# Experts of a mixture layer: weight splits and a step's small operations in program order on ScalarE and VectorE

## The chip, the cores and the metric

The kernel runs on one core of a Trainium2 chip. The metric is the time of one execution on the device, in microseconds (us); of several runs the median is given. TensorE is called PE here, VectorE DVE, ScalarE ACT, GpSimd POOL and SyncE SP, as in the profile; PEld is PE's loading of weights.

## The reference

A network of two blocks on 256 tokens of width 1024: in each a mixer (retention, then banded attention), a feed-forward part and a small per-layer embedding. The first feed-forward part is dense. The second, with which the change deals, is a mixture of eight experts with 3584 hidden columns, of which each token uses two:

```python
logits = (xn @ w_router).astype(jnp.float32)
top_v, top_i = lax.top_k(logits, TOP_K)
top_w = jax.nn.softmax(top_v, axis=-1)
gates = jnp.sum(jax.nn.one_hot(top_i, N_EXPERTS) * top_w[..., None], axis=-2)
for e in range(N_EXPERTS):
    y = y + gates[..., e:e + 1] * swiglu(xn, w_gate[e], w_up[e], w_down[e])
# swiglu: (silu(x @ w_gate) * (x @ w_up)) @ w_down
```

Inputs, weights and output are float32.

## The kernel before, in words

**Weights and their splits.** PE multiplies in a format of fewer bits than float32, so each operand is split into a high and a low part, and a product is the sum of three products (`mm3`, L341 to L345): high by high, low by high, high by low. All weights come as one stream (class `Stream`). Its chunks of 1 MB are loaded by SP into raw buffers (`wraw`): four at first, and `widen` adds three and then four more, so eleven in the experts. Each chunk makes two parts of 128 x 1024. A part is split by `_split` (L277 to L295): ACT copies the raw values into `whi` (L288), and DVE subtracts that from the raw values into `wlo` (L289). Five pairs of split buffers (`HL = 5`) are there. The last expert's parts are split in two halves of 128 x 512.

`get` (L297 to L306) is called for the chunks that the next matmuls need. It gives out splits until the part that stands five behind the first part asked for has its turn, so that splits run ahead of use:

```python
        while self.n_hl < min(max(end, at + self.hl_bufs), len(self.parts)):
            self._split()
```

**An expert.** `experts` (L997 to L1093) runs over experts 0 to 7 and, in each, over 14 steps j of 256 hidden columns. The tokens of an expert are first gathered into slots. A *wide* expert (0, 2, 3, 5, 6) has 128 slots, and its products are those three. A *narrow* expert (1, 4, 7) has 64 slots, whose high and low parts stand beside each other as 64 + 64 columns of one operand, so two products per weight do (L1012, L1013). A step does this:

1. Up product: two chunks (`eu`, four parts) into a PSUM bank `mm`, gate and up columns side by side; 24 matmuls in a wide expert, 16 in a narrow one.
2. Down product of the step before: one chunk (`ed`, two parts) into the two `acc` banks; 12 or 8 matmuls.
3. `turned` (L1025 to L1056). Wide: ACT's silu into `sg` (L1031), DVE's multiplication (L1032), two transposes on PE into `tp` (L1038), and a split of the result into `hh` (ACT, L348) and `hl` (DVE, L349), by `split_psum`. Narrow: ACT copies the bank into `cp` (L1043), PE folds high and low halves by eight small matmuls into `tp` (L1048), ACT's silu (L1052), DVE's multiplication (L1053) into `sgn`, and the split, both halves into one tile `hh`.

The split (with the silu, in a narrow expert) is held back as the closure `split` and called in the next step, behind the first call of `get` there (L1061 to L1064). At step 13 the tokens of the next pair of experts may be gathered, the last two down chunks are used, and the sum goes back to the tokens, weighted by the gates (L1082 to L1093).

**What sets the order.** The program's text gives each instruction a priority by its place, and the framework's planner orders each engine's instructions: among those that by its own timetable can run it takes the earliest in the program. That timetable is made before the kernel runs, and the order of each engine is fixed by it; on the chip an engine runs its instructions in that order and waits by semaphores. `after` (L443 to L445) adds a dependence without a semaphore: it only forces the planner to place one instruction behind another. SP's queue holds the loads, which `fill` issues as raw buffers come free; POOL has next to nothing to do in the experts.

By the program's text a step's order on ACT and DVE is this, with p and p+1 for the two parts of the down chunk of step j-1: the splits up to p+4, then `cp` or `sg` of step j, then splits p+5 and p+6 (the next `get`), then the held-back closure of step j. Parts p+2 to p+5 are up parts of step j+1 and p+6 and p+7 the down parts of step j.

Of the kernel before, what the change touches and what calls it, by code (L numbers as in the profile page):

```python
# [11 lines left out]
F32 = mybir.dt.float32  # L12
# [4 lines left out]
ALU = mybir.AluOpType  # L17
# [210 lines left out]
class Stream:  # L228


    def __init__(self, prog, plans, raw_bufs, hl_bufs, raw_pool, hl_pool):
        self.nc = prog.nc
        self.items, self.parts, self.first = [], [], []
        for ap, plan in plans:
            offs, _ = offsets(plan)
            for c, o in zip(plan, offs):
                self.first.append(len(self.parts))
                step = max(c.kt // 2, 1)
                self.parts += [(len(self.items), k, step) for k in range(0, c.kt, step)]
                self.items.append((ap, c, o))  # L240
        self.expert = prog.expert
        self.first.append(len(self.parts))
        self.free = {raw_pool: raw_bufs}
        self.base, self.extra = raw_pool, []
        self.hl_pool, self.hl_bufs = hl_pool, hl_bufs
        self.raw, self.hl = {}, {}
        self.n_raw = self.n_hl = self.n_get = 0
# [29 lines left out]
    def _split(self):  # L277
        i, k, nk = self.parts[self.n_hl]
        c = self.items[i][1]
        self.fill()  # L280
        t, pool = self.raw[i]
        f = nk * c.n
        hi, lo = (self.hl_pool.tile([P, 1024], F32R, name=n) for n in ("whi", "wlo"))
        n = 1 if c.key[0] in ("eu", "ed") and c.key[1] < NE - 1 else 2
        for i0 in range(0, f, f // n):
            h, l = (x[:, i0:i0 + f // n] for x in (hi, lo))
            src = t[:, k * c.n + i0:k * c.n + i0 + f // n]
            self.nc.scalar.activation(h, src, AF.Copy)  # L288
            self.nc.vector.tensor_tensor(l, src, h.bitcast(F32), op=ALU.subtract)  # L289
        if k + nk == c.kt:  # L290
            self.free[pool] += 1
            del self.raw[i]
        self.hl[self.n_hl] = [x[:, :f].rearrange("p (k n) -> p k n", n=c.n) for x in (hi, lo)]
        self.n_hl += 1
        self.fill()  # L295

    def get(self, *keys):  # L297

        at = self.first[self.n_get]
        for key in keys:  # L300
            assert self.items[self.n_get][1].key == key, (self.items[self.n_get][1].key, key)
            self.n_get += 1
        end = self.first[self.n_get]
        while self.n_hl < min(max(end, at + self.hl_bufs), len(self.parts)):
            self._split()
        return [[x[:, k, :] for x in self.hl[i]] for i in range(at, end) for k in range(self.parts[i][2])]  # L306


class Program:
    RAW, HL = 4, 5  # L310

    def __init__(self, tc, io, stop=None, dump=None):
        self.tc, self.nc, self.io = tc, tc.nc, io
        self.stop, self.dump_ap = stop, dump
        self.fence, self.in_set = [], []
        self.turns = {}
        self.expert = {}


# [24 lines left out]
        mm(out, l[0], r[1], start=False, stop=False)  # L344
        mm(out, l[1], r[0], start=False, stop=stop)  # L345

    def split_psum(self, hi, lo, ps):
        self.nc.scalar.activation(hi, ps, AF.Copy)  # L348
        self.nc.vector.tensor_tensor(lo, ps, hi.bitcast(F32), op=ALU.subtract)  # L349

    def gain_row(self, ap, n=D, name="gain", pool=None, engine=None):
        t = (pool or self.gains).tile([P, n], F32, name=name)
# [644 lines left out]
    def experts(self, px, pool, gates, slot, w, first, wide):  # L997
# [5 lines left out]
        for e in range(NE):  # L1003
# [21 lines left out]
            def turned(j, ps):  # L1025


                hh = pool.tile([P, 2, P], F32R, name="hh", bufs=2)
                if wide[e]:
                    sg = self.work.tile([P, 256], F32, name="sg", tag="xs", bufs=3)  # L1030
                    nc.scalar.activation(sg, ps[:, :256], AF.Silu)  # L1031
                    nc.vector.tensor_tensor(sg, sg, ps[:, 256:], op=ALU.mult)  # L1032
                    hT[j] = (hh, pool.tile([P, 2, P], F32R, name="hl", bufs=2))

                    def turn():
                        tp = self.bank("tp")
                        for k in range(2):
                            nc.tensor.transpose(tp[:, k * P:(k + 1) * P], sg[:, k * P:(k + 1) * P], self.ident)  # L1038
                        return lambda: self.split_psum(*hT[j], tp[:, :256].rearrange("p (k s) -> p k s", k=2))
                    return turn  # L1040
                hT[j] = (hh,)
                cp = self.work.tile([P, 512], F32, name="cp", tag="xs", bufs=3)
                nc.scalar.activation(cp, ps, AF.Copy)  # L1043

                def turn():
                    tp = self.bank("tp")[:, :256].rearrange("p (c s) -> p c s", s=64)
                    for c in range(4):
                        nc.tensor.matmul(tp[:, c], cp[:, c * P:(c + 1) * P], self.fold, start=True, stop=True)  # L1048

                    def split():  # L1050
                        sg = self.work.tile([P, 2, 64], F32, name="sgn", tag="xs", bufs=3)
                        nc.scalar.activation(sg, tp[:, :2], AF.Silu)  # L1052
                        nc.vector.tensor_tensor(sg, sg, tp[:, 2:], op=ALU.mult)  # L1053
                        self.split_psum(hh[:, :, :64], hh[:, :, 64:], sg)
                    return split
                return turn  # L1056

            split = None
            for j in range(nj):
                ps = self.bank("mm")  # L1060
                for k0 in (0, 4):  # L1061
                    wu = w.get(("eu", e, j, k0 * P))
                    if split:
                        split()  # L1064
                        split = None
                    for k in range(4):
                        product(ps, [a[:, k0 + k, :] for a in xg], wu[k],
                                k0 + k == 0, k0 + k == KD - 1)
                rows = rows_of(j - 1) if 0 < j < nj - 1 else []
                if j == nj - 1:  # L1070
                    if e + 1 in groups:
                        have.update(self.gather(px, pool, slot, groups[e + 1], wide))
                    rows = rows_of(nj - 2, nj - 1)
                    turn = turned(j, ps)
                    down(rows[:2])
                    turn()()
                    down(rows[2:], True)
                else:
                    turn = turned(j, ps)
                    down(rows)  # L1080
                    split = turn()
            with self.tc.high_priority(offset=300) if e == NE - 1 else nullcontext():  # L1082
                for n in range(2):
                    spare = n and e == NE - 1
# [10 lines left out]
    def moe_layer(self):  # L1095
        nc, tc, io = self.nc, self.tc, self.io
        with self.pool("moex") as px, self.pool("moe") as pool:
            with self.banks(acc="67", mm="45", tp="01", ps="23"):
                rows = [px.tile([P, NB, D], F32, name="xg", tag="xgl"), px.tile([P, KD, T], F32, name="xnT", tag="xgh")]
                with self.banks(mm="45", tp="45"):  # L1100
                    quarter = self.ple_up(1, self.pl1, pool)
                    for n in range(2):
                        quarter(0, n)
                with tc.high_priority(offset=300):
                    slot, weigh = self.router(*rows)
                    first = self.gather(px, pool, slot, GROUPS[0], WIDE)
                with tc.issue_after(self.logits.ins):
                    quarter(1, 0)
                    quarter(1, 1)
                gates, slot, load = weigh()  # L1110
                self.lb = self.lower_bounds(pool)
                most = nc.values_load(load[0:1, 0:1], min_val=0, max_val=P + T)
                self.experts(px, pool, gates, slot, self.w, first, WIDE)
        self.wide.close()
        with tc.If(most > P):
            with self.pool("moe2") as pool, self.pool("raw2", 2) as raw, \
                    self.pool("hl2", 4) as hl, self.banks(acc="67", mm="45", tp="01", ps="23"):
                again = Stream(self, [(self.we, plan_expert(i)) for i in range(NE)], 2, 4, raw, hl)
                nc.vector.tensor_tensor(slot, slot, self.turn[:, None, 1].to_broadcast([P, NB, NE]), op=ALU.subtract)
                wide = (True,) * NE  # L1120
                self.experts(pool, pool, gates, slot, again, self.gather(pool, pool, slot, GROUPS[0], wide), wide)
        self.routed.close()
        return self.at("e")

# [487 lines left out]
```

## Time and profile before

| | |
|---|---|
| median of 3 runs | 2432.98 us (2430.64 to 2434.96) |
| profiled execution | 2430.28 us, its span 2428.5 us, granted clock of PE 0.996 |
| PE busy | 2369.9 us, 98% of the span |
| DVE busy | 1892.6 us, 78% |
| ACT busy | 1567.7 us, 65% |
| weight load (PEld) busy | 1972.4 us, 81% |
| DMA | 605.72 MB, 249 GB/s over the span |
| experts | from about 575 to 1538 us of the span |

Busy shares are averages over stages with different limits, so a stage is read by its own stretch. An idle time of an engine has a releaser: the instruction of another engine, or the DMA, whose end let it go on. A matmul's end is modelled; from one matmul's start to the next is the better measure. In the timeline a row may stand for several instructions of one kind in a row (x2), and the time is then that of all.

### The profile page before, as it was taken

The numbers are of one execution on the slowest core, as the hardware profiler recorded it, in microseconds if no ns is written. First come the engines' busy times: TensorE is split into PE (matmuls) and PEld (weight loads), VectorE is DVE, ScalarE is ACT, GpSimd is POOL, SyncE is SP. The second block draws the span as 40 slices with busy tenths as digits, with TensorE's granted clock in tenths as the row PEclk, the third lists the DMA queues.
The fourth block names the chain that finished last, engine by engine and source line by source line (L and its number), as shares of the span: only waits on it lengthen the run. The fifth ranks groups of instructions, "written<-read, shape, count | busy, mean of one in ns | idle before, by whom it ended". The sixth has DMA issues, their size and how long they took to land. (4 is left out here: it accounts for less than half of the span.)

```text
span 2428.5 us, 35659 instructions
## 1 busy us (share of the span) xinstructions
PE 2369.9 (98%) x13032; PEld 1972.4 (81%) x13032; DVE 1892.6 (78%) x3026; ACT 1567.7 (65%) x2609; POOL 61.1 (3%) x105
## 2 busy tenths in 40 slices
PE   8999999999999999999999999899999999999999
PEld 6978998887876787876788876698789989878998
DVE  6756567778999889899998899878776567877655
ACT  6446555667888777778777789645755554575554
POOL 0000000000000000000000000100000000100000
PEclk9999999999999999999999999999999999999999
DMA  7445555567989998999999999534345554434553
GB/s 286 167 174 208 191 191 191 194 247 265 369 333 394 360 359 335 359 356 409 356 369 343 364 356 393 148 132 161 133 167 199 189 173 139 170 126 177 194 189 107
DMA packets 88393, 605.72 MB, mean 249 GB/s; under 512 B 10480, under 2 KB 12144, under 8 KB 17296
## 3 DMA queue, kind: packets, MB, share of 16 engines
q1 hardware_dynamic: 85792, 593.91, 65.4%
q0 software_dynamic: 2416, 9.44, 1.7%
q8 instruction: 104, 1.70, 0.3%
q14 instruction: 81, 0.66, 0.1%
HBM read 602.26 MB, written 1.05 MB: 248 GB/s over the span
## 5 line engine op out<-in xcount | busy, mean ns | idle before, releaser
L289 DVE TENSOR_TENSOR wlo<-wraw,whi 128x512 fp32r<-128x512 f32 (+1 forms) x1656 | 1383.4, 876 | 369.4 <-ACT whi L288 356.1
L288 ACT ACTIVATE whi<-wraw 128x512 fp32r<-128x512 f32 (+1 forms) x1656 | 1204.1, 776 | 438.9 <-PE mm L344 201.9
L343 PE MATMUL mm<-xth,whi 128*128 128x256 f32 x1296 | 366.3, 283 | 0.0
L345 PE MATMUL mm<-xth,wlo 128*128 128x256 f32 x1296 | 364.0, 281 | 1.2 <-DVE wlo L289 1.2
L344 PE MATMUL mm<-xtl,whi 128*128 128x256 f32 x1296 | 364.2, 281 | 0.0
L345 PEld LDWEIGHTS mm<-xth,wlo 128*128 128x128 f32 x1296 | 247.1, 191 | 2.1 <-DVE wlo L289 1.4
L343 PEld LDWEIGHTS mm<-xth,whi 128*128 128x128 f32 x1296 | 243.6, 188 | 4.9 <-issue 3.0
L344 PEld LDWEIGHTS mm<-xtl,whi 128*128 128x128 f32 x1296 | 243.8, 188 | 3.7 <-issue 2.1
L344 PE MATMUL acc<-wlo,hh 128*128 128x512 f32 x624 | 243.6, 390 | 0.0
L345 PE MATMUL acc<-whi,hl 128*128 128x512 f32 x624 | 243.5, 391 | 0.0
L343 PE MATMUL acc<-whi,hh 128*128 128x512 f32 x624 | 231.6, 391 | 1.5 <-ACT hh L348 1.5
L343 PE MATMUL mm<-whi,xth 128*128 128x512 f32 (+2 forms) x592 | 231.7, 391 | 0.6 <-ACT whi L288 0.4
L344 PE MATMUL mm<-wlo,xth 128*128 128x512 f32 (+2 forms) x592 | 231.5, 391 | 0.3 <-DVE wlo L289 0.3
L345 PE MATMUL mm<-whi,xtl 128*128 128x512 f32 (+2 forms) x592 | 229.5, 388 | 0.5 <-DVE xtl L349 0.5
L343 PE MATMUL mm<-whi,xgh 128*128 128x512 f32 x560 | 226.2, 404 | 2.6 <-ACT whi L288 2.6
L344 PE MATMUL mm<-wlo,xgh 128*128 128x512 f32 x560 | 223.8, 400 | 3.0 <-DVE wlo L289 3.0
L345 PE MATMUL mm<-whi,xgl 128*128 128x512 f32 x560 | 222.2, 397 | 0.0
L1013 PE MATMUL mm<-wlo,xgh 128*128 128x512 f32 x336 | 143.2, 426 | 5.2 <-DVE wlo L289 4.4
L343 PEld LDWEIGHTS acc<-whi,hh 128*128 128x128 f32 x624 | 117.1, 188 | 26.4 <-ACT hh L348 3.3
L345 PEld LDWEIGHTS acc<-whi,hl 128*128 128x128 f32 x624 | 117.1, 188 | 25.0 <-DVE hl L349 0.6
L344 PEld LDWEIGHTS acc<-wlo,hh 128*128 128x128 f32 x624 | 117.2, 188 | 23.4 <-DVE wlo L289 0.3
L1012 PE MATMUL mm<-whi,xgh 128*128 128x512 f32 x336 | 134.4, 400 | 0.0
(386 smaller groups left out, 3091.7 us busy)
## 6 DMA issues: line engine op xcount, KB each, us to landing
wraw<-in_we_dram SPq DMA_DIRECT2D x336, 1024.0 KB, 5.8
wraw<-in_w_dram SPq DMA_DIRECT2D x218, 1024.0 KB, 4.8
wraw<-in_w_dram SPq DMA_DIRECT2D x4, 912.0 KB, 4.7
wraw<-in_w_dram SPq DMA_DIRECT2D x6, 512.0 KB, 3.6
bias<-in_rel_rows_dram POOLq DMA_DIRECT2D x4, 768.0 KB, 4.6
gain<-in_norm_ffn_dram POOLq DMA_DIRECT2D x2, 512.0 KB, 6.6
gn<-in_ret_gn_dram SPq DMA_DIRECT2D x4, 256.0 KB, 3.2
gain<-in_norm_ple_dram POOLq DMA_DIRECT2D x2, 512.0 KB, 6.6
```

The costliest lines, as they stand in the source:

```text
L288: self.nc.scalar.activation(h, src, AF.Copy)
L289: self.nc.vector.tensor_tensor(l, src, h.bitcast(F32), op=ALU.subtract)
L343: mm(out, l[0], r[0], start=start, stop=False)
L344: mm(out, l[0], r[1], start=False, stop=False)
L345: mm(out, l[1], r[0], start=False, stop=stop)
L1012: nc.tensor.matmul(out, x[0], wk[0], start=start, stop=False)
L1013: nc.tensor.matmul(out, x[0], wk[1], start=False, stop=stop)
```

## The change

The splits of expert weights, `cp`, silu, multiplications, `hh` and `hl` of all steps are now chained by `inorder`: on ACT, and apart from that on DVE, each is placed behind the one that stands before it in the program's text (`after`, so no semaphore). `get` takes a list `between`; behind each split that it makes it calls the first closure left, and the rest behind the last split. A wide expert has one closure (hh and hl), a narrow one two (silu and multiplication; then hh). In the program's text hh and hl of a wide expert so stand behind split p+5, a narrow expert's silu behind p+5 and its hh behind p+6. PE's, SP's and POOL's instructions are not chained, nor are the gather, `ohT`, and the sums back to the tokens. The chain is begun anew behind the experts.

```diff
--- before.py
+++ after.py
@@ -229,7 +229,7 @@
 
 
     def __init__(self, prog, plans, raw_bufs, hl_bufs, raw_pool, hl_pool):
-        self.nc = prog.nc
+        self.prog, self.nc = prog, prog.nc
         self.items, self.parts, self.first = [], [], []
         for ap, plan in plans:
             offs, _ = offsets(plan)
@@ -285,8 +285,10 @@
         for i0 in range(0, f, f // n):
             h, l = (x[:, i0:i0 + f // n] for x in (hi, lo))
             src = t[:, k * c.n + i0:k * c.n + i0 + f // n]
-            self.nc.scalar.activation(h, src, AF.Copy)
-            self.nc.vector.tensor_tensor(l, src, h.bitcast(F32), op=ALU.subtract)
+            act = self.nc.scalar.activation(h, src, AF.Copy)
+            dve = self.nc.vector.tensor_tensor(l, src, h.bitcast(F32), op=ALU.subtract)
+            if c.key[0] in ("eu", "ed"):
+                self.prog.inorder(act=act, dve=dve)
         if k + nk == c.kt:
             self.free[pool] += 1
             del self.raw[i]
@@ -294,8 +296,10 @@
         self.n_hl += 1
         self.fill()
 
-    def get(self, *keys):
-
+    def get(self, *keys, between=()):
+
+
+        between = list(between)
         at = self.first[self.n_get]
         for key in keys:
             assert self.items[self.n_get][1].key == key, (self.items[self.n_get][1].key, key)
@@ -303,6 +307,10 @@
         end = self.first[self.n_get]
         while self.n_hl < min(max(end, at + self.hl_bufs), len(self.parts)):
             self._split()
+            if between:
+                between.pop(0)()
+        for step in between:
+            step()
         return [[x[:, k, :] for x in self.hl[i]] for i in range(at, end) for k in range(self.parts[i][2])]
 
 
@@ -313,7 +321,7 @@
         self.tc, self.nc, self.io = tc, tc.nc, io
         self.stop, self.dump_ap = stop, dump
         self.fence, self.in_set = [], []
-        self.turns = {}
+        self.turns, self.line = {}, {}
         self.expert = {}
 
 
@@ -344,9 +352,17 @@
         mm(out, l[0], r[1], start=False, stop=False)
         mm(out, l[1], r[0], start=False, stop=stop)
 
-    def split_psum(self, hi, lo, ps):
-        self.nc.scalar.activation(hi, ps, AF.Copy)
-        self.nc.vector.tensor_tensor(lo, ps, hi.bitcast(F32), op=ALU.subtract)
+    def split_psum(self, hi, lo, ps, inorder=False):
+        act = self.nc.scalar.activation(hi, ps, AF.Copy)
+        dve = self.nc.vector.tensor_tensor(lo, ps, hi.bitcast(F32), op=ALU.subtract)
+        if inorder:
+            self.inorder(act=act, dve=dve)
+
+    def inorder(self, **ins):
+
+        for e, i in ins.items():
+            self.after(i, [self.line[e]] if e in self.line else [])
+            self.line[e] = i
 
     def gain_row(self, ap, n=D, name="gain", pool=None, engine=None):
         t = (pool or self.gains).tile([P, n], F32, name=name)
@@ -1028,41 +1044,39 @@
                 hh = pool.tile([P, 2, P], F32R, name="hh", bufs=2)
                 if wide[e]:
                     sg = self.work.tile([P, 256], F32, name="sg", tag="xs", bufs=3)
-                    nc.scalar.activation(sg, ps[:, :256], AF.Silu)
-                    nc.vector.tensor_tensor(sg, sg, ps[:, 256:], op=ALU.mult)
+                    self.inorder(act=nc.scalar.activation(sg, ps[:, :256], AF.Silu),
+                                 dve=nc.vector.tensor_tensor(sg, sg, ps[:, 256:], op=ALU.mult))
                     hT[j] = (hh, pool.tile([P, 2, P], F32R, name="hl", bufs=2))
 
                     def turn():
                         tp = self.bank("tp")
                         for k in range(2):
                             nc.tensor.transpose(tp[:, k * P:(k + 1) * P], sg[:, k * P:(k + 1) * P], self.ident)
-                        return lambda: self.split_psum(*hT[j], tp[:, :256].rearrange("p (k s) -> p k s", k=2))
+                        return [lambda: self.split_psum(*hT[j], tp[:, :256].rearrange("p (k s) -> p k s", k=2), True)]
                     return turn
                 hT[j] = (hh,)
                 cp = self.work.tile([P, 512], F32, name="cp", tag="xs", bufs=3)
-                nc.scalar.activation(cp, ps, AF.Copy)
+                self.inorder(act=nc.scalar.activation(cp, ps, AF.Copy))
 
                 def turn():
                     tp = self.bank("tp")[:, :256].rearrange("p (c s) -> p c s", s=64)
                     for c in range(4):
                         nc.tensor.matmul(tp[:, c], cp[:, c * P:(c + 1) * P], self.fold, start=True, stop=True)
 
-                    def split():
-                        sg = self.work.tile([P, 2, 64], F32, name="sgn", tag="xs", bufs=3)
-                        nc.scalar.activation(sg, tp[:, :2], AF.Silu)
-                        nc.vector.tensor_tensor(sg, sg, tp[:, 2:], op=ALU.mult)
-                        self.split_psum(hh[:, :, :64], hh[:, :, 64:], sg)
-                    return split
+                    sg = self.work.tile([P, 2, 64], F32, name="sgn", tag="xs", bufs=3)
+
+                    def silu():
+                        self.inorder(act=nc.scalar.activation(sg, tp[:, :2], AF.Silu),
+                                     dve=nc.vector.tensor_tensor(sg, sg, tp[:, 2:], op=ALU.mult))
+                    return [silu, lambda: self.split_psum(hh[:, :, :64], hh[:, :, 64:], sg, True)]
                 return turn
 
-            split = None
+            steps = []
             for j in range(nj):
                 ps = self.bank("mm")
                 for k0 in (0, 4):
-                    wu = w.get(("eu", e, j, k0 * P))
-                    if split:
-                        split()
-                        split = None
+                    wu = w.get(("eu", e, j, k0 * P), between=steps)
+                    steps = []
                     for k in range(4):
                         product(ps, [a[:, k0 + k, :] for a in xg], wu[k],
                                 k0 + k == 0, k0 + k == KD - 1)
@@ -1073,12 +1087,13 @@
                     rows = rows_of(nj - 2, nj - 1)
                     turn = turned(j, ps)
                     down(rows[:2])
-                    turn()()
+                    for step in turn():
+                        step()
                     down(rows[2:], True)
                 else:
                     turn = turned(j, ps)
                     down(rows)
-                    split = turn()
+                    steps = turn()
             with self.tc.high_priority(offset=300) if e == NE - 1 else nullcontext():
                 for n in range(2):
                     spare = n and e == NE - 1
@@ -1112,6 +1127,7 @@
                 most = nc.values_load(load[0:1, 0:1], min_val=0, max_val=P + T)
                 self.experts(px, pool, gates, slot, self.w, first, WIDE)
         self.wide.close()
+        self.line = {}
         with tc.If(most > P):
             with self.pool("moe2") as pool, self.pool("raw2", 2) as raw, \
                     self.pool("hl2", 4) as hl, self.banks(acc="67", mm="45", tp="01", ps="23"):
@@ -1119,6 +1135,7 @@
                 nc.vector.tensor_tensor(slot, slot, self.turn[:, None, 1].to_broadcast([P, NB, NE]), op=ALU.subtract)
                 wide = (True,) * NE
                 self.experts(pool, pool, gates, slot, again, self.gather(pool, pool, slot, GROUPS[0], wide), wide)
+        self.line = {}
         self.routed.close()
         return self.at("e")
```

## Rows read from the trace of the kernel before

**Rows 1.** Busy time by stretch: experts 1, 4, 5 (wide), 7; first line names columns.

```profile
core 0: us, PE busy (x) PEld busy (x) DVE busy (x) ACT busy (x) POOL busy (x), PEclk, DMA share, GB/s
704.07:797.05 92.98, 83.24 (x384) 63.15 (x385) 87.13 (x97) 78.44 (x106) 0.00 (x0) 1.00 1.00 397
1070.24:1163.20 92.96, 88.90 (x393) 62.78 (x394) 88.98 (x98) 82.73 (x113) 0.00 (x0) 1.00 1.00 405
1204.50:1290.00 85.50, 85.50 (x381) 69.34 (x380) 77.58 (x82) 64.61 (x80) 0.00 (x0) 1.00 0.96 368
1431.48:1523.36 91.88, 89.52 (x385) 58.61 (x386) 91.80 (x171) 87.48 (x182) 0.00 (x0) 1.00 0.92 371
```

**Rows 2.** Timeline of a step in expert 4: ACT, DVE, PE.

```profile
1101.24 0.60 ACT L1043 ACTIVATE cp<-mm 128x512 f32<-128x512 f32 x1 [0.42 <-PE mm L1013]
...
1104.10 0.28 ACT L1052 ACTIVATE sgn<-tp 128x128 f32<-128x128 f32 x1 [0.37 <-PE tp L1048]
1104.27 2.00 ACT L288 ACTIVATE whi<-wraw 128x1024 fp32r<-128x1024 f32 x2
...
1108.77 0.60 ACT L1043 ACTIVATE cp<-mm 128x512 f32<-128x512 f32 x1 [0.41 <-PE mm L1013]
...
1105.36 2.36 DVE L289 TENSOR_TENSOR wlo<-wraw,whi 128x1024 fp32r<-128x1024 f32 x2
1107.63 0.28 DVE L349 TENSOR_TENSOR hh<-sgn,hh 128x128 fp32r<-128x128 f32 x1
1107.84 2.35 DVE L289 TENSOR_TENSOR wlo<-wraw,whi 128x1024 fp32r<-128x1024 f32 x2
...
1103.51 0.55 PE L1048 MATMUL tp<-fold,cp 128*128 128x64 f32 x4
...
1106.64 0.50 PE L1013 MATMUL mm<-wlo,xgh 128*128 128x512 f32 x1 [0.21 <-DVE wlo L289]
1106.98 0.39 PE L1012 MATMUL mm<-whi,xgh 128*128 128x512 f32 x1
```

**Rows 3.** Waits, 800 to 1500 us: total us, times, longest.

```profile
DVE wlo L289 <- ACT whi L288: 43.1, 105, 1.3
...
ACT whi L288 <- DMA wraw<-in_we_dram: 1.1, 2, 0.8
```

**Rows 4.** Expert 1: DVE's hh in all, then timeline of ACT, DVE, PE.

```profile
L349 DVE TENSOR_TENSOR hh<-sgn,hh 128x128 fp32r<-128x128 f32 x13 | 3.8, 289 | 4.5 <-ACT hh L348 4.5
...
724.03 0.28 ACT L1052 ACTIVATE sgn<-tp 128x128 f32<-128x128 f32 x1
724.60 4.15 ACT L288 ACTIVATE whi<-wraw 128x1024 fp32r<-128x1024 f32 x4 [0.29 <-PE mm L1012]
...
728.98 0.29 DVE L349 TENSOR_TENSOR hh<-sgn,hh 128x128 fp32r<-128x128 f32 x1 [0.97 <-ACT hh L348]
...
723.00 1.00 PE L1048 MATMUL tp<-fold,cp 128*128 128x64 f32 x8
...
729.33 0.50 PE L1012 MATMUL acc<-whi,hh 128*128 128x512 f32 x1 [1.54 <-DVE hh L349]
```

**Rows 5.** Timeline of a step in expert 0: ACT's sg, PE's transposes.

```profile
623.50 0.37 ACT L1031 ACTIVATE sg<-mm 128x256 f32<-128x256 f32 x1
...
625.31 0.39 PE L1038 MATMUL tp<-ident,sg 128*128 128x128 f32 x2
```

**Rows 6.** Timeline of a wide step in expert 5: ACT, DVE, PE.

```profile
1204.97 0.38 ACT L348 ACTIVATE hh<-tp 128x256 fp32r<-128x256 f32 x1 [0.67 <-PE tp L1038]
1205.25 2.00 ACT L288 ACTIVATE whi<-wraw 128x1024 fp32r<-128x1024 f32 x2
...
1206.34 1.23 DVE L289 TENSOR_TENSOR wlo<-wraw,whi 128x1024 fp32r<-128x1024 f32 x1 [0.25 <-ACT whi L288]
...
1204.32 0.40 PE L345 MATMUL acc<-whi,hl 128*128 128x512 f32 x1
1204.55 0.38 PE L1038 MATMUL tp<-ident,sg 128*128 128x128 f32 x2
```

## The prediction

> **What bounds the kernel now.** I read the experts stage first, because every line of the diff acts there alone: busy time by stretch, one stretch per kind of expert [rows 1]. In ten steps of a wide expert TensorE (PE) is busy for all of 85.50 us, VectorE (DVE) for 77.58: a wide step is 8.55 us and PE sets it. In twelve steps of the narrow experts it is otherwise. In expert 7 DVE is busy 91.80 of 91.88 us. In experts 1 and 4 it is busy 87.13 of 92.98 and 88.98 of 92.96, so that it stood still for 5.85 and 3.98 us, and PE has idle time there too. In a queue one wlo takes DVE (1107.63 - 1105.36) / 2 = 1.135 us, and hh 0.21, as long as mul: 6 x 1.135 + 0.4 = **7.2 us of DVE work** against narrow steps of 1108.77 - 1101.24 = 7.53 [rows 2].
>
> Then the waits [rows 3]: from 800 to 1500 us DVE's wlo waits 43.1 us for ACT's whi, 105 times, and whi waits twice, 1.1 us in all, for a load. So loads limit nothing. Last the order on each engine. I number the splits by parts: with p and p+1 the down weights of step j-1, p+2 to p+5 are the up weights of step j+1, p+6 and p+7 the down weights of step j. By the program cp (wide: sg) of step j stands behind split p+4, since the call of get before it splits five parts ahead. Early in expert 1 and in expert 0 cp and sg stand there [rows 4, 5]. Early in expert 1 ACT does silu at 724.03, then four whi, then hh, but DVE does its hh three splits earlier in its own order: at 728.98 it waits 0.97 for ACT's hh, and PE waits 1.54 for DVE's at 729.33 [rows 4]; DVE's wait at hh is 4.5 us over the expert. From expert 1's step 8 on, and in expert 4, cp comes three splits early: two whi, silu, two whi, hh [rows 2]. That disagreement between two planned orders is what the change abolishes.
>
> **The change, part by part.** It adds no instruction, DMA or semaphore. ACT's and DVE's lists in the experts are pinned to program order; SP's loads, POOL and PE's matmuls are not.
>
> *DVE's wait at hh in expert 1.* Silu goes behind p+5 and hh behind p+6 on both engines. The 5.8 us of idle time go, if all else stays: at most from 7.75 a step to 7.3. Taken: -4.5 us, in the seven early steps.
>
> *PE's own order.* This is the term that decides. The planner gives PE each matmul by program order among those that its timetable says can run. Why did it move cp up three splits in expert 4? Program order has p+2 to p+4 first, their buffers are free, and their data is there: ACT never waits for a load [rows 3]. The eleven raw buffers hold 22 parts, over three steps. Only a timetable in which the **loads arrive late** explains an order that passes three splits for cp. In expert 0, which starts with full raw buffers, and in expert 1 until the eighth step, it does not pass them, as such a timetable would have it [rows 4, 5].
>
> Now cp has to stand behind whi p+4, so in the timetable it waits for a load one and a half chunks on. While cp waits, the timetable's PE does what is ready: the up matmuls of p+2 and p+3, and one of p+4. The fold follows only then: 2 x 4 + 1 = nine up matmuls behind down instead of being mixed into it. In a wide expert, sg waits likewise and its mul waits for wlo p+4: transposes follow 2 x 6 + 3 = fifteen up matmuls, where now they come directly behind down [rows 6]. The chip then follows that PE order though its data is early. What such a step takes, walked from rows:
>
> Narrow: fold to silu 1.03 (eight in a row, 723.00 to 724.03) [rows 4]; silu to whi p+6 0.17 [rows 2]; whi to wlo 1.09 and the last wlo below 1.23 [rows 6]; wlo to hh 1.135; hh 0.2; then three wlo, since the fold stands behind the last matmuls of the third split from there, 2 x 1.135 + 1.23 = 3.50; wlo to its matmul 0.05 (1105.36 + 1.23 to 1106.64); four matmuls, the first 0.34 (1106.64 to 1106.98), then 3 x 0.23 = 1.03 [rows 2]. Sum **8.20 us** against 7.53: +0.67. DVE idles 1 us of each step, because silu, on which mul and whi p+6 queue, waits for a late fold.
>
> Wide: transposes to hh 0.42; hh to whi p+6 0.28; whi to wlo 1.09 [rows 6]; wlo 1.23; to its matmul 0.05; eleven down and fifteen up matmuls, 0.34 + 25 x 0.23 = 6.09. Sum **9.16 us** against 8.55: +0.61. This hangs on the count: with fourteen up matmuls it is 8.93, with twelve 8.47, under PE's 8.55, and so nothing.
>
> Sum: wide experts 2, 3, 5, 6 pass the splits from their third or fourth step, 40 steps x 0.61 = +24.4. Expert 4: 12 x 0.67 = +8.0. Expert 1 from its eighth step: 5 x 0.67 = +3.4, less 4.5. Expert 7, in halves: the same walk with halves of 0.6 us leaves DVE's 2 x 1.2 + 0.2 of lead longer than the path fold, silu, half a whi (about 2.5), so nothing to +0.3 a step; taken +1.5. Expert 0: 0, it runs in program order already [rows 5]. Ends of experts: PE waits 1 to 2 us there now; bounds -2 and +2 in all, taken 0. **Sum +33 us** on the profiled execution's own 2430.28 (span 2428.5), 2463; the median of the runs is 2.7 above that execution: **2466 us**.
>
> Bounds: nothing shows the timetable itself. Below, fourteen wide and eight narrow matmuls: 40 x 0.38 + 12 x 0.44 + 5 x 0.44 - 4.5 = +18. Above, sixteen wide and ten narrow: 40 x 0.84 + 17 x 0.9 + 12 x 0.3 - 4.5 = +48. Own range of this case 2450 to 2482.
>
> **The rivals.** *The waits vanish and nothing replaces them: faster.* If the timetable's loads are on time, PE keeps fold and transposes within four or five matmuls of down, as early in expert 1, where the fold stands directly behind down at 723.00 [rows 4]. Narrow steps then fall to DVE's 7.3: expert 1 gives 5.2, expert 4 3.4, expert 7 nothing since DVE is full [rows 1], the ends 1.5: -10 us, **2423**. It turns where the fold comes more than five up matmuls behind down. For it: those early steps ran in just this ACT order. Against: it leaves unexplained why cp passed three splits whose data was there.
>
> *The pinned order changes nothing because buffers, not order, make the gaps: about 2433, up to 2447.* The repeated gap would come from the five split buffers; ACT would be as far ahead as they allow, in either order. Against it: the gap's releaser is ACT's hh and whi, not a buffer that comes free, and DVE, which stands still, would have to be waiting for PE [rows 4]. Here too falls the case that losses of half the size meet expert 1's gain.
>
> That rival is a rule of the Trainium skill, page "Perfetto Trace Analysis", section "Optimization Strategy": a same gap repeating on the engine that should be full can mean that there is too little SBUF or PSUM for the next tile. By that rule the sum would be about 0; this case's releasers speak for the order instead (0.97 us for ACT's hh).
>
> *Transposes without cover.* In a wide step mul queues behind wlo p+4; were it late when down ends, transposes that stand directly behind down would stall PE 0.15 to 0.35 a step, 65 steps, +10 to +23. That gives much the same time by another wait (PE on DVE's sg), and lies inside the range; it counts with the first case.
>
> **How the numbers follow.** Late turns on PE 0.68; waits vanish 0.23; no change or a small loss 0.09. A measurement tells about 0.2%, 4.9 us, from no change. Faster: the second case, 0.23. Same: half of the third and the far end of the first, 0.06. Slower: 0.71. The range has to reach from the likeliest case's upper end into the faster case to leave out no more than 2 in 10: 2421 to 2484.
>
> **What would show it.** Right: in the timeline of PE after the change, nine up matmuls between down and the fold, fourteen to sixteen between down and the transposes; narrow steps of about 8.2 and wide of about 9.1 us; DVE's wait at wlo for whi up by 0.6 to 1 us per step, and ACT waiting for the fold or the transposes. The faster rival: fold right behind down, narrow steps of 7.3, DVE busy over 97% of experts 1 and 4. The third: steps as now with other instructions at the gaps. Wrong altogether if wide steps stay at 8.55 while PE's transposes do come late: then some slack of ACT that I left out carries them. Wrong, too, if loads start to be waited for: slower steps free raw buffers later, but they also need them later.

## The result and the profile after

The changed kernel takes 2459.92 us (2459.01 to 2462.17, four runs) against 2432.83 (2430.64 to 2434.96, four runs): the ratio is 1.0113, its 95% interval 1.0101 to 1.0126. It is slower by 27 us. The profiled execution of after took 2462.17 us with a span of 2460.4; against the span of before that is +31.9, since the one is the slowest of its four runs and the other below its median.

All of it lies in the experts. This table has the time from an expert's first `cp` or `sg` on ACT to the next expert's first, and for expert 7 to the last sum back to the tokens (575.0 to 1537.9 us before, 575.6 to 1570.3 after):

| expert | 0 w | 1 n | 2 w | 3 w | 4 n | 5 w | 6 w | 7 n |
|---|---|---|---|---|---|---|---|---|
| before, us | 122.3 | 116.0 | 128.5 | 121.8 | 114.3 | 123.5 | 124.5 | 111.8 |
| after, us | 123.8 | 113.0 | 132.9 | 127.0 | 122.0 | 128.4 | 128.1 | 119.6 |
| difference | +1.5 | -3.0 | +4.4 | +5.2 | +7.7 | +4.9 | +3.6 | +7.8 |

The same view of busy time by stretch as [rows 1], of after: twelve steps of experts 1 and 4 (in 4 the last holds a gather), ten of the wide expert 5, twelve of expert 7.

```profile
core 0: us, PE busy (x) PEld busy (x) DVE busy (x) ACT busy (x) POOL busy (x), PEclk, DMA share, GB/s
708.95:800.85 91.90, 84.13 (x383) 61.57 (x382) 87.79 (x97) 80.50 (x109) 0.00 (x0) 1.00 1.00 408
1082.10:1182.80 100.70, 87.09 (x403) 64.04 (x401) 91.35 (x101) 82.52 (x115) 0.00 (x0) 1.00 0.99 385
1219.90:1309.90 90.00, 88.89 (x385) 69.18 (x383) 76.61 (x81) 63.42 (x82) 0.00 (x0) 1.00 0.91 351
1461.40:1559.40 98.00, 83.50 (x386) 60.98 (x385) 93.86 (x170) 86.69 (x182) 0.00 (x0) 1.00 0.85 331
```

DVE was busy for 88.98 of 92.96 us in expert 4, and is for 91.35 of 100.70 now. In expert 7 it was never idle, and is idle for 4.1 of 98.0 us. The wide stretch, in which PE had no gap, is 90.00 us long instead of 85.50. PE's idle time is only 1.1 us of that: in the timeline a matmul lasts 0.39 or 0.40 us and the next one starts 0.23 us behind its start, so that most of a late start does not show as idle time.

Now a narrow step, in the timeline of expert 4; it answers to [rows 2]. The lines are 8 to 17 further down than before (fold L1064, silu L1069, mul L1070, hh L356 and L357).

```profile
1121.60 0.40 PE L1028 MATMUL mm<-whi,xgh 128*128 128x512 f32 x1
...
1123.85 0.40 PE L1028 MATMUL mm<-whi,xgh 128*128 128x512 f32 x1
1124.09 1.00 PE L1064 MATMUL tp<-fold,cp 128*128 128x64 f32 x8
...
1127.86 0.50 PE L1028 MATMUL acc<-whi,hh 128*128 128x512 f32 x1 [1.11 <-DVE hh L357]
...
1132.30 0.89 PE L1064 MATMUL tp<-fold,cp 128*128 128x64 f32 x7
...
1125.12 0.28 ACT L1069 ACTIVATE sgn<-tp 128x128 f32<-128x128 f32 x1 [1.57 <-PE tp L1064]
1125.30 1.05 ACT L288 ACTIVATE whi<-wraw 128x1024 fp32r<-128x1024 f32 x1
...
1125.43 0.29 DVE L1070 TENSOR_TENSOR sgn<-sgn,tp 128x128 f32<-128x128 f32 x1 [0.16 <-ACT sgn L1069]
1126.38 1.23 DVE L289 TENSOR_TENSOR wlo<-wraw,whi 128x1024 fp32r<-128x1024 f32 x1 [0.66 <-ACT whi L288]
1127.52 0.28 DVE L357 TENSOR_TENSOR hh<-sgn,hh 128x128 fp32r<-128x128 f32 x1
1127.73 5.76 DVE L289 TENSOR_TENSOR wlo<-wraw,whi 128x1024 fp32r<-128x1024 f32 x5
```

Nine up matmuls run from 1121.60 to 1123.85, one row each, and the fold comes only behind them, at 1124.09; before it was mixed into down. Silu waits for it on ACT (1.57 us). Behind silu on ACT stands the next whi, so DVE, which has done all its splits, waits 0.16 us for silu and then 0.66 for that whi. Its hh comes at 1127.52, and PE has been waiting 1.11 us for it at 1127.86. From fold to fold it is 1132.30 - 1124.09 = 8.21 us.

A wide step in expert 5, answering to [rows 6]:

```profile
1250.65 0.38 PE L1054 MATMUL tp<-ident,sg 128*128 128x128 f32 x2
...
1252.97 0.63 PE L351 MATMUL acc<-whi,hh 128*128 128x512 f32 x2
1253.72 0.50 PE L352 MATMUL acc<-wlo,hh 128*128 128x512 f32 x1
...
1259.61 0.38 PE L1054 MATMUL tp<-ident,sg 128*128 128x128 f32 x2
...
1251.07 0.39 ACT L356 ACTIVATE hh<-tp 128x256 fp32r<-128x256 f32 x1 [2.64 <-PE tp L1054]
1251.35 4.84 ACT L288 ACTIVATE whi<-wraw 128x1024 fp32r<-128x1024 f32 x5
...
1251.49 0.42 DVE L357 TENSOR_TENSOR hl<-tp,hh 128x256 fp32r<-128x256 f32 x1 [0.80 <-ACT hh L356]
1252.44 5.77 DVE L289 TENSOR_TENSOR wlo<-wraw,whi 128x1024 fp32r<-128x1024 f32 x5 [0.52 <-ACT whi L288]
```

The transposes stood directly behind down; they stand fifteen up matmuls behind now. ACT's hh waits 2.64 us for them, with the next whi behind it; DVE waits 0.80 for hh and 0.52 for whi, and the first matmul of down that needs the new wlo comes late (at 1253.72; two matmuls of 0.23 behind 1252.97 would be 1253.43). From transposes to transposes: 8.96 us. The view of waits from 800 to 1500 us, with total, times and longest, shows the same in sum:

```profile
ACT hh L356 <- PE tp L1054: 142.0, 56, 3.4
DVE wlo L289 <- ACT whi L288: 37.7, 72, 1.3
DVE hl L357 <- ACT hh L356: 37.6, 44, 1.5
PEld acc L1028 <- DVE hh L357: 26.8, 20, 1.6
```

Before, the first was 43.0 us in 54 times, the second 43.1 us in 105 [rows 3], the third 1.3 us in 2, the fourth 1.8 us in 2.

### The profile page after: what moved, and what is told of

It is laid out like the page before. It is cut to its first block, busy times and chain, and to the rows that moved or that the text cites. A ratio compares the mean times of both kernels' runs of the same rounds, so it can differ in the third digit from the quotient of the medians.

```text
span 2460.4 us, 35707 instructions
## 1 busy us (share of the span) xinstructions
PE 2377.0 (97%) x13032; PEld 1971.3 (80%) x13032; DVE 1890.4 (77%) x3026; ACT 1551.9 (63%) x2609; POOL 61.4 (2%) x105
## 3 DMA queue, kind: packets, MB, share of 16 engines
HBM read 602.26 MB, written 1.05 MB: 245 GB/s over the span
## 5 line engine op out<-in xcount | busy, mean ns | idle before, releaser
L352 PE MATMUL acc<-wlo,hh 128*128 128x512 f32 x624 | 248.7, 399 | 3.9
L352 PEld LDWEIGHTS acc<-wlo,hh 128*128 128x128 f32 x624 | 117.5, 188 | 43.1 <-DVE wlo L289 20.0
```

## The experiments

The theory is the prediction's: the planner, which holds the loads to be late, places PE's fold and transposes late, and the chip follows. The main rival was that the pinned order of ACT and DVE costs the time by itself, wherever PE's fold stands. Each edit is made to the changed kernel; the first four runs stand beside a median of 2431.26 us of the kernel before, the last four beside 2430.27.

**Half of each load.** Edit:

```diff
-    self.nc.sync.dma_start(t[:, :f], src[:, o:o + P * f]...)
+    g = f // 2
+    self.nc.sync.dma_start(t[:, :g], src[:, o:o + P * g]...)
...
+    at = (k * c.n) % (c.kt * c.n // 2) if c.key[0] in ("eu", "ed") else k * c.n
-    src = t[:, k * c.n + i0:k * c.n + i0 + f // n]
+    src = t[:, at + i0:at + i0 + f // n]
```

> The changed kernel with expert weight loads of 512 KB instead of 1 MB: the second half of each chunk is left out, and both parts of a chunk are split from the first half, so the same instructions run on PE, ACT and DVE on other data. Loads did not limit the chip, so the shorter loads matter only to the planner's timetable. Theory (the pinned cp and sg wait for late loads in the timetable, and PE's fold and transposes are therefore placed late): with loads early in the timetable the fold stands five up matmuls behind down instead of nine, the transposes one instead of fifteen (after a run-in of some steps); narrow steps 7.29 us, wide 8.55, about 2428 us. Rival (the pinned order on ACT and DVE costs the time by itself, wherever PE's fold stands): steps stay at 8.2 and 8.96, 2460 us. Rival (too few split buffers): also 2460, as the buffers are the same.

Measured: 2416.24 us (ratio to before 0.9938, 0.9922 to 0.9955). Eleven narrow steps of expert 4 and eight wide ones of expert 5, busy time by stretch with the columns as above:

```profile
1060.10:1140.30 80.20, 77.33 (x358) 57.38 (x357) 80.20 (x89) 74.34 (x101) 0.00 (x0) 1.00 0.65 217
1203.40:1271.80 68.40, 68.40 (x306) 55.17 (x305) 62.55 (x65) 54.27 (x66) 0.00 (x0) 1.00 0.55 191
```

Narrow steps take 80.20 / 11 = 7.29 us with DVE busy throughout, wide ones 8.55. The pinned order on ACT and DVE is the same as in the change, and so are the buffers: what differs for the order, which is fixed before the run, is what the planner believes of the loads, with PE's order as its consequence (in the trace the fold stands five up matmuls behind down; the transposes come closer to down by two matmuls a step, until only one is between). Both rivals fall. Nor is it needed that the shorter loads helped the steps on the chip itself: the next two runs, with full loads, reach 8.55 in wide steps and 7.29 in narrow ones. The 12 us below what was expected lie outside the steady steps: the stage begins 2.6 us earlier, and the transitions are shorter.

**cp and sg one get earlier.** Edit:

```diff
+                if j < nj - 1:
+                    turn = turned(j, ps)
                 rows = rows_of(j - 1) if 0 < j < nj - 1 else []
...
                 else:
-                    turn = turned(j, ps)
                     down(rows)
```

> The changed kernel with cp or sg (and the wide multiplication) of a step pinned behind split p+2 instead of p+4, by calling turned ahead of the get of the down weights; all else is pinned as in the change, the narrow silu behind p+5 and hh behind p+6 too. Theory: in the timetable cp no longer waits for a load that is one and a half chunks on, so the fold and the transposes stand directly or up to three matmuls behind down; narrow steps 7.29, wide 8.55 with at most 0.15 more where the transposes have no cover: 2420 to 2430 us, faster than both kernels. Rival (the pinned order by itself): silu, hh and the splits are still in that order, so narrow steps stay near 8.2 and wide near 8.96: 2450 to 2460 us.

Measured: 2423.02 us (0.9966, 0.9953 to 0.9978), with loads of full size. Ten narrow steps of expert 4, five wide ones of expert 5:

```profile
1065.90:1140.00 74.10, 68.40 (x322) 52.59 (x321) 73.92 (x81) 66.57 (x92) 0.00 (x0) 1.00 1.01 417
1188.00:1230.70 42.70, 42.70 (x191) 34.72 (x190) 39.22 (x42) 32.45 (x40) 0.00 (x0) 1.00 0.98 364
```

As the theory has it: the place of cp, sg and the wide multiplication, two splits earlier, is worth about 35 us (27 us slower than the kernel before against 8 us faster). Narrow steps are 7.40 rather than 7.29.

**PE in program order too.** Edit: each matmul of up and down, the transposes and the folds go through `self.inorder(pe=...)`; for instance

```diff
-                        nc.tensor.matmul(tp[:, c], cp[:, c * P:(c + 1) * P], self.fold, start=True, stop=True)
+                        self.inorder(pe=nc.tensor.matmul(tp[:, c], cp[:, c * P:(c + 1) * P], self.fold, start=True, stop=True))
```

> The changed kernel with PE's up, down, fold and transpose matmuls chained in program order as well, so that fold and transposes stand directly behind down; ACT and DVE are pinned as in the change. Theory: narrow steps fall to DVE's 7.29. Wide steps fall from 8.96, but as mul is behind wlo p+4 and nothing covers the transposes, each may cost 0.15 to 0.35 over 8.55: 2425 to 2440 us. Rival (the pinned order on ACT and DVE costs it by itself): 2450 to 2460 us.

Measured: 2436.08 us (1.0019, 1.0009 to 1.0029). Ten narrow steps of expert 4, ten wide ones of expert 5:

```profile
1073.30:1146.30 73.00, 67.83 (x324) 53.51 (x322) 73.00 (x81) 67.67 (x92) 0.00 (x0) 1.00 1.01 418
1190.30:1277.90 87.60, 87.58 (x381) 68.54 (x380) 78.35 (x80) 69.16 (x81) 0.00 (x0) 1.00 0.94 357
```

ACT and DVE have the order of the change to the letter, cp behind p+4 included, with PE's order alone put right: 22 us of the 27 are gone (it is 4.8 above its median of the kernel before), and narrow steps are 7.29. What is left is in the wide steps, 8.76 us each. The timeline of PE and DVE shows it:

```profile
1200.44 0.39 PE L1025 MATMUL acc<-whi,hl 128*128 128x512 f32 x1
1200.82 0.44 PE L1057 MATMUL tp<-ident,sg 128*128 128x128 f32 x2
...
1200.35 0.41 DVE L1051 TENSOR_TENSOR sg<-sg,mm 128x256 f32<-128x256 f32 x1
```

The last matmul of down starts at 1200.44 and the transposes could start at 1200.67; mul ends at 1200.76 and they start at 1200.82, 0.15 late; their row is 0.44 long where it was 0.38 [rows 6]. That is the uncovered transpose, 0.21 us a step. Over 65 steps it is 14 us that DVE's pinned order, with mul behind wlo p+4, does cost by itself; the narrow experts win 7 of them back.

**Narrow experts alone.** Edit: splits, sg, mul and hh of wide experts are not chained.

```diff
-            if c.key[0] in ("eu", "ed"):
+            if c.key[0] in ("eu", "ed") and not WIDE[c.key[1]]:
                 self.prog.inorder(act=act, dve=dve)
```

> The changed kernel with only the narrow experts' splits and small operations pinned; wide experts are left to the planner. Theory: wide steps are 8.55 again and lose their 18 to 20 us, the narrow experts keep theirs (about -3 in expert 1, +8 in 4, +8 in 7): 2440 to 2447 us. Rival (the loss sits in how narrow and wide experts meet, at the ends of experts): most of the 27 us stay, 2455 to 2460 us.

Measured: 2441.19 us (1.0042, 1.0025 to 1.0059). Nine narrow steps of expert 4, ten wide ones of expert 5:

```profile
1080.50:1154.00 73.50, 63.49 (x287) 46.39 (x288) 66.07 (x72) 59.34 (x82) 0.00 (x0) 1.00 0.98 380
1199.30:1284.80 85.50, 85.50 (x381) 69.37 (x380) 76.97 (x81) 62.78 (x78) 0.00 (x0) 1.00 0.97 364
```

Wide steps are 8.55 again, narrow ones 8.2; the wide experts take within 1 us of what they took before.

**DVE alone.** Edit: `inorder` chains DVE only.

```diff
-        for e, i in ins.items():
+        for e, i in [(e, i) for e, i in ins.items() if e == "dve"]:
```

> The changed kernel with the pinned order on DVE alone; ACT is the planner's. Theory: a narrow cp is ACT's alone, so in the timetable it goes ahead of the late splits again and the fold stands directly behind down: narrow steps about 7.3. A wide step's mul is on DVE behind wlo p+4 still, so the transposes stay behind fifteen up matmuls: about 8.9. 2433 - 5 - 3 + 18: 2440 to 2446 us. Rival (what costs is ACT's queue, silu and whi behind a waiting instruction): wide steps fall to 8.55 and the time to 2425.

Measured: 2454.54 us (1.0098, 1.0083 to 1.0114), a miss: 8.5 us above the range expected. Wide steps came out as expected, 8.95, with the transposes behind fifteen up matmuls: there DVE's mul alone holds them back. Narrow steps were 7.2 in the first part of expert 1 as expected, but 8.2 behind it and in expert 4, with the fold directly behind down. ACT and DVE in expert 4:

```profile
1126.03 0.31 ACT L356 ACTIVATE hh<-sgn 128x128 fp32r<-128x128 f32 x1 [0.73 <-DVE sgn L1070]
...
1130.37 0.28 ACT L1069 ACTIVATE sgn<-tp 128x128 f32<-128x128 f32 x1 [0.70 <-PE tp L1064]
...
1128.75 2.36 DVE L289 TENSOR_TENSOR wlo<-wraw,whi 128x1024 fp32r<-128x1024 f32 x2 [0.21 <-ACT whi L288]
1131.62 2.36 DVE L289 TENSOR_TENSOR wlo<-wraw,whi 128x1024 fp32r<-128x1024 f32 x2 [0.51 <-ACT whi L288]
```

Here the two orders disagree, as they did in expert 1 before the change [rows 4], the other way round: ACT has silu and hh where the planner put them, and waits 0.70 us for the fold and 0.73 for DVE's mul, which stands further down in DVE's pinned order; the whi behind them come late, and DVE waits 0.21 and 0.51 for those. So a late fold is one way to 8.2, and disagreeing orders are another.

**All closures behind p+6.** Edit:

```diff
             self._split()
-            if between:
-                between.pop(0)()
```

> The changed kernel without what places the closures one each behind the next splits: silu, mul and hh of a narrow step, and hh and hl of a wide one, all stand behind p+6, and the rest is pinned as in the change. Theory: with mul directly ahead of hh on DVE, hh waits for ACT's hh, which waits for mul: about 0.28 + 0.30 of idle DVE per narrow step. Where the fold is early (expert 1) the narrow steps rise from 7.29 to 7.8 or 7.9; where it is late, a third split covers DVE's wait for the fold, so 8.2 stays or falls to 7.9. Wide: one split more between the transposes and whi p+7 takes the late transposes off the path, 8.55 to 8.96. 2440 to 2460 us. Rival (the places of silu and hh cost nothing): 2460.

Measured: 2460.93 us (1.0122, 1.0106 to 1.0137), the time of the change by another distribution. Ten narrow steps of expert 4, eight wide ones of expert 5:

```profile
1083.40:1167.60 84.20, 74.19 (x321) 50.88 (x320) 73.88 (x81) 67.15 (x91) 0.00 (x0) 1.00 0.96 369
1242.40:1310.80 68.40, 68.40 (x306) 55.59 (x305) 61.30 (x65) 50.76 (x65) 0.00 (x0) 1.00 0.97 364
```

Narrow steps are 8.42 in all three narrow experts, but for a few of 8.6 to 8.9, more than expected; DVE in expert 1 shows why:

```profile
744.64 0.28 DVE L1068 TENSOR_TENSOR sgn<-sgn,tp 128x128 f32<-128x128 f32 x1
745.30 0.29 DVE L355 TENSOR_TENSOR hh<-sgn,hh 128x128 fp32r<-128x128 f32 x1 [0.38 <-ACT hh L354]
746.25 6.91 DVE L289 TENSOR_TENSOR wlo<-wraw,whi 128x1024 fp32r<-128x1024 f32 x6 [0.66 <-ACT whi L288]
```

hh waits 0.38 us for ACT's hh, as expected, and the wlo behind it another 0.66, because the next whi stands behind that hh on ACT: that second wait I had left out. Wide steps are 8.55 though the transposes still stand fifteen up matmuls behind down: with hh behind whi p+6, that whi no longer waits for the late transposes. It takes both to make the wide loss, the late transposes and an hh ahead of whi p+6. And placing silu and hh one each behind the next two splits is worth having: in the first steps of expert 1, where the fold stands five up matmuls late with it and four without, a step is 7.29 against 8.43.

**The best of them.** First the narrow experts pinned on ACT, DVE and PE, wide ones free. Edit: that of the run with narrow experts alone, and the narrow matmuls and folds chained as well.

```diff
-                    nc.tensor.matmul(out, x[0], wk[1], start=False, stop=stop)
+                    self.inorder(pe=nc.tensor.matmul(out, x[0], wk[1], start=False, stop=stop))
```

> Pinned are the narrow experts alone, on ACT and DVE as in the change and on PE as well (fold directly behind down); wide experts are the planner's, as in the kernel before. Theory: narrow steps 7.29 in all of experts 1 and 4 and 7.63 in 7, wide 8.55. Against the run with the narrow experts pinned on ACT and DVE alone (2441) that takes off 5 x 0.92 in expert 1, 11 x 0.92 in expert 4 and 11 x 0.57 in expert 7: 2420 us, 11 us below the kernel before. Rival (folds without up matmuls ahead of them wait for cp, and give it back): 2425 to 2430.

Measured: 2423.49 us (0.9968, 0.9956 to 0.9980). The steps are as expected, 7.29 and 7.63, but experts 4 and 2 take 1.8 and 1.4 us more than before, in their last steps. In expert 4 a fold waits 2.12 us for cp, as the rival had it. Behind that wait the profile has TensorE at the lower of its two clock levels (granted clock 0.50, 1.2 GHz) for 3.4 us:

```profile
1150.80 1.73 PE L1064 MATMUL tp<-fold,cp 128*128 128x64 f32 x8 [2.12 <-ACT cp L1059]
...
1151.10:1154.50 3.40, 3.40 (x13) 2.99 (x12) 2.54 (x4) 2.50 (x5) 0.00 (x0) 0.50 1.00 424
```

Expert 2 is wide and has no cp. There PE waits 1.47 us for a wlo, and 3.4 us at a granted clock of 0.50 follow (from 925.8); before the change the same wait was 1.48 us, and the clock stayed at 1.00. So a difference of a microsecond or two at the end of an expert is not the order's alone. Then sg and mul of the wide experts one get earlier, the narrow experts pinned on all three engines:

```diff
+                if j < nj - 1 and wide[e]:
+                    turn = turned(j, ps)
                 rows = rows_of(j - 1) if 0 < j < nj - 1 else []
...
                 else:
+                    if not wide[e]:
+                        turn = turned(j, ps)
                     down(rows)
...
-                    nc.tensor.matmul(out, x[0], wk[0], start=start, stop=False)
+                    self.inorder(pe=nc.tensor.matmul(out, x[0], wk[0], start=start, stop=False))
```

> All experts pinned on ACT and DVE, sg of the wide experts behind split p+2 as in the run with cp early, cp of the narrow behind p+4 with PE pinned there too. Theory: wide 8.55, narrow 7.29 against the 7.40 of the run with cp early: 23 steps x 0.11 less than its 2423, 2420 us. Rival (the ends of the experts, not the steps, make up the rest): 2423 or more.

Measured: **2419.76 us** (0.9953, 0.9939 to 0.9966), 10.5 us below the kernel before and about 38 below the change, each taken against its own median of the kernel before. Eleven narrow steps, ten wide ones:

```profile
1064.70:1145.00 80.30, 73.86 (x354) 58.98 (x355) 80.30 (x89) 74.43 (x101) 0.00 (x0) 1.00 1.01 419
1183.50:1268.90 85.40, 85.40 (x381) 69.39 (x380) 77.51 (x82) 64.71 (x80) 0.00 (x0) 1.00 0.97 369
```

DVE is busy for all of the narrow stretch and PE for all of the wide one.

## Why the prediction was right, and where not

The step that decided, **PE's own order**, held to the matmul: nine up matmuls ahead of the fold in expert 4 and in expert 1 from its eighth or ninth step, fifteen ahead of the transposes. Its cause held as well: with shorter loads the planner puts both early again, and with cp two splits earlier too. The timetable itself is in no trace; these runs show that the length of the loads and the place of cp decide.

The terms of the sum, as predicted and as measured in the trace of after:

- **Narrow step**: 8.20 worked out, 8.21 measured. Expert 4: +8.0, measured +7.7.
- **Expert 1**: -1.1, measured -3.0. The early steps fell to 7.29, and the loss of the late ones is near what was worked out; the 1.9 us between lie in its first and last step, for which the sum took 0.
- **Wide step**: 9.16 worked out, 8.96 measured. The walk took the order within down as high by high, then low by high. The planner put the second high-by-high matmul ahead of the first that needs the new wlo (the row of two at 1252.97), so the loop holds one matmul less: 9.16 - 0.23 = 8.93. Experts 2, 3, 5 and 6 give +18.1 instead of +24.4; each also has a run-in of four or five steps rather than three, in which the count is not yet fifteen (nine to fourteen behind its first step). Expert 0 gave +1.5 where I took 0. It has a run-in of ten to two matmuls, but that is not shown to be the cause: the run with cp early has none in expert 0 and takes 1.3 us more there too.
- **Expert 7**: +1.5 taken, +7.8 measured. This term failed, and the overlap behind it: I held DVE's lead to be long enough to hide the fold. I carried the count of nine over from the whole splits. With half splits the planner placed eleven up matmuls ahead of the fold, from 1492.39 to 1494.99:

```profile
1492.39 0.40 PE L1028 MATMUL mm<-whi,xgh 128*128 128x512 f32 x1
...
1494.99 0.40 PE L1028 MATMUL mm<-whi,xgh 128*128 128x512 f32 x1
1495.23 1.00 PE L1064 MATMUL tp<-fold,cp 128*128 128x64 f32 x8
...
1498.64 0.50 PE L1028 MATMUL acc<-whi,hh 128*128 128x512 f32 x1 [1.20 <-DVE hh L357]
...
1496.57 0.29 DVE L1070 TENSOR_TENSOR sgn<-sgn,tp 128x128 f32<-128x128 f32 x1 [0.17 <-ACT sgn L1069]
1497.09 1.29 DVE L289 TENSOR_TENSOR wlo<-wraw,whi 128x512 fp32r<-128x512 f32 x2 [0.23 <-ACT whi L288]
```

The fold then follows a wlo half that comes later in DVE's order, its lead over mul is shorter, and DVE waits 0.17 us for silu and 0.23 for whi; mul to the next wlo takes 0.52 instead of 0.20. The step is 8.20 instead of 7.63. My upper bound, 0.3 a step, was too low. In the run with short loads, with seven up matmuls, expert 7's steps were 7.63.

So the sum, +33, met the measured span's +31.9 partly because expert 7's miss (+6.3) and the wide experts' (-6.3) cancelled, which is luck. The median came out 6 us below the 2466, inside the range of the likeliest case: between the medians the change is +27 us, 5 less than between the two profiled executions on which the sum was made. One sign named in the prediction did not come: DVE's wait at wlo for whi did not rise in sum (43.1 us before, 37.7 after). The new waits of the wide steps are ACT's hh for the transposes and DVE's hl for that hh.

Of the rivals: the faster one had its mechanism right and its condition wrong. Where the fold stands within five up matmuls of down, ACT and DVE agree, and silu and hh stand behind one split each, the steps are 7.29, as in expert 1's first eight and in four of the experiments (7.40 with cp early, 8.42 without the splits between); the planner did not leave it there. The buffers are excluded: the kernel of 2419.76 us has the same five pairs, and in both of its stretches shown the engine that sets the step has no gap left; the releasers had named the order. The Trainium skill, page "Perfetto Trace Analysis", section "Optimization Strategy", has it that a gap that repeats can mean too little SBUF or PSUM for the next tile. These gaps were not of that kind. The transposes without cover are real at 0.21 us a step, inside the 0.15 to 0.35 given, but only where PE is pinned: in the change itself PE waits for sg at the transposes once from 800 to 1500 us, for 0.5 us.

## What to carry to other kernels

A pinned order on some engines is an input to the planner of the others: ask where the pinned instruction now stands in the planner's timetable, wrong as that may be, and which free engine's instructions move with it. Put an instruction whose result another engine waits for ahead of work that the planner believes late. How many engines are pinned decided less: all three gave 2436 us, ACT and DVE alone with cp and sg earlier 2423, and DVE alone, with ACT's order left to disagree, 2455. When a wait of one engine looks small, walk the loop that it closes: once PE's order was known, the narrow and the wide step could be worked out to within 0.2 us by adding start-to-start times around the loop of releasers.

## What was not expected of the hardware

In the kernel of 2419.76 us the loads run at a DMA share of 1.01 and 419 GB/s in the narrow steps, 426 GB/s in the last 60 us of that stretch (1085 to 1145). Three chunks in 7.29 us are 3 x 1.0486 MB / 7.29 = 431.5 GB/s, which is slightly more than arrives, so these steps use up some of the lead that the raw buffers hold. Yet no instruction of the experts is shown waiting for a weight load in this run: from a load's landing to the first whi of its chunk there are 28 us early in expert 1 and still 14 us at its end, and the last six steps hold that level. Whether a longer row of narrow experts would come to be limited by loads is not shown.

And a row's releaser can mislead: the wlo at 1118.17, in the step before the one shown, has its 0.66 us put down to a load's DMA, though a whi ended just before it (1117.09 + 1.05 = 1118.14); the same wait in the next step, at 1126.38, is put down to ACT's whi.
